# Loads of the gate vectors and of the S5 readout moved to the queue of POOL, with seven gate pairs ahead of the first projection in place of five and the readout's steps spread further

## The chip, the cores and the metric

The kernel runs on one core of a Trainium2 chip. A core has five engines that run their own instruction streams in order: PE (matrix products, with a separate loader for the stationary operand), DVE (element-wise work), ACT (activations and copies), POOL (element-wise work, general) and SP (here it only starts DMA transfers). Sixteen DMA engines are shared by all queues. An engine that starts a transfer puts it on its own queue and goes on; an engine that meets an instruction whose data isn't there stops, with all that stands behind it. The metric is the device time of one execution in microseconds (us); lower is better.

## The reference

One layer of a generator's backbone, on 512 latent tokens and 256 context tokens, width 2048. Cut to its core:

```python
s_c = silu(c)
mx = split(s_c @ w_ada + b_ada, 6)            # 6 vectors of 2048: the adaLN rows
h_lat = modulate(rms_norm(x, g_pre_mix), mx[0], mx[1])
u_lat = h_lat @ w_in                          # first projection, 512 x 2048 x 2048
y = sum of two directions of s5_readout(s5_scan(u_lat[..., 1536:]))   # SSM heads, 512 channels
ssm = gelu(y + d * u); ssm = ssm * sigmoid(ssm @ w_glu)
mix_lat = concat([multiscale_pool(u_lat[..., :1536]), ssm]) @ w_out
x = x + mx[2] * rms_norm(mix_lat, g_post_mix)
f_lat = conv_glu_ffn(modulate(rms_norm(x, g_pre_ffn), mx[3], mx[4]), w_up, w_conv, w_down)
x = x + mx[5] * rms_norm(f_lat, g_post_ffn)
```

`mx[2]` to `mx[5]` are called the gates here. They are products of a vector with a matrix of 2048 columns each, and nothing but the silu of `c` goes into them, so the kernel may compute them whenever there is room.

## The kernel before

Weights are fp32 and come as pages of 128x1024 (512 KB). Each page is split into a rounded part and a remainder: the DMA brings `raw` (issued by SP, L60), ACT makes `whi` (L77), DVE makes `wlo` (L78), and PE runs three matmuls per tile (`mm3`, L176 to L178). `raw`, `whi` and `wlo` have two buffers each, so PE can only start a page when DVE has written its `wlo`. A page that PE uses for 24 matmuls of 512 columns is the usual unit; the text counts pages from the first of the first projection, which is page 8 (pages 8 to 31 first projection `ub`, 32 to 39 pooling, 40 to 60 output projection `wo`, 61 and 62 the GLU weights `glu`, then the rest of the output projection, `wo2`/`wq`, up to page 73).

Work that isn't weights is written as generators and threaded between the pages by a planner (class `Threads`): `tick` is called a few times per page, and lets each generator go on while the page it asked for has come and while the charge of its steps (`yield charge, lag`) fits into 0.76 of the time ticked. So the tables of charges and lags set the order of the instructions, which is then fixed on every engine. `bg.finish(t)` emits all that is left of a generator at one place.

The two generators that matter:

- `gemv` computes three of the gates. One step takes a page `gv` of 128x1024 of the matrix (`gvload`, L172, two buffers, loaded two products ahead) and multiplies it on DVE into a sum (L943). The first `2 * NGP` of these products are done ahead, in the adaLN stage, from loads of 1 MB (`gpair_load`, `gpair_dot`, L607). `gfin` closes a gate (L953 to L959). A second generator loads 32 pages for the fourth gate during the MLP, with the same `gvload`.
- The readout of the SSM runs in `scan`, after the states are ready, in eight units u = 0 to 7. For each: six POOL operations build a table `cl` (`cl_build`, L562 and L564, after a small L786); ACT copies parts of it into `R` (`window`, L797 to L799); PE makes `eb` (L821) and ACT copies it to `E` (L823); DVE adds `du` to a part of `E` (L827); ACT's queue writes `E` to DRAM (`e_scratch`, L828); the queue reads it back in another layout as `Mi` (L810); PE makes `yb` from `cl` and `Mi` (`y_unit`, L760 to L762), ACT applies the gelu (L763); after each second unit PE transposes (`ytp`, L772), and ACT and DVE make `yTr` (L777, L778).

`second_half()` emits the GLU matmuls at page 61 and calls `bg.finish` on what is left of the readout first. Behind the output projection, the normalisation for the MLP (`norm_pair`, from L1056 on) calls `bg.finish` on `gemv` before it forms the MLP's input `hf` and `h` (L1125 to L1130), since that uses two of the gates (`acol`). Then come the MLP's matmuls `up` and `dn`.

Of the kernel before, what the change touches and what calls it, by code (L numbers as in the profile page):

```python
# [129 lines left out]
def emit(tc, A, out, xs_dram, dbg=None):  # L130
    nc = tc.nc
    V, S, PO, PE = nc.vector, nc.scalar, nc.gpsimd, nc.tensor
# [7 lines left out]
    e_dram = nc.dram_tensor("e_scratch", (8, 32, 960), F32, kind="Internal").ap()  # L140
# [19 lines left out]
    def pg(name, shape=(1024,), dt=F32, parts=128):  # L160
        return shaped(sb.tile([128, 1024], dt, name=name, tag="pg", bufs=NPG), shape, slice(0, parts))

    def bank(name, cols=512, parts=128):
        t = ps.tile([128, 512], F32, name=name, tag="bank")
        return t[:parts, :cols]
# [3 lines left out]

    def gvload(ap, q=None):  # L170
        r = ring.tile([128, 1024], F32, name="gv", tag="gv", bufs=2)
        nc.sync.dma_start(r[:], ap)  # L172
        return r

    def mm3(o, ahi, alo, bhi, blo, start, stop):
# [253 lines left out]
    def at(r, f):  # L429
        rounds.setdefault(r, []).append(f)  # L430
# [169 lines left out]
    def gpair_load(nt):  # L600
        gpair[nt] = p0.tile([128, 2, 1024], F32, name="adag", tag="adak", bufs=3)
        nc.sync.dma_start(gpair[nt][:], A["ada_n"][0, nt].rearrange("a p n -> p a n"))

    def gpair_dot(nt):
        g = gpair.pop(nt)
        for hf in range(2):
            V.scalar_tensor_tensor(scr[:], g[:, hf], 1.0, srow[:, hf * 1024:(hf + 1) * 1024], op0=OP.mult,  # L607
                                   op1=OP.mult, accum_out=gacc[:, hf, 0, nt:nt + 1])

    NGP = 5  # L610
    at(31, cond_rows)
    for nt, r in enumerate((34, 36, 38, 40, 42)):
        at(r, lambda nt=nt: gpair_dot(nt))
    for nt, r in enumerate((32, 33, 34, 36, 38)):
        at(r, lambda nt=nt: gpair_load(nt))
    at(4, lambda: W.load(2))
    at(6, lambda: W.make(2))
# [62 lines left out]
    def front():  # L680
# [5 lines left out]
        for gb in range(4):  # L686
# [5 lines left out]
                                        ap=[[768, 8], [6144, 16], [1, 768]]), uc.rearrange("p i c -> p (i c)"))  # L692
        mi_next(NMT)
        yield 0.0, 1.2
        for gb in range(4):
            u = pg(f"UT{gb}", (8, NCH))
            UT[gb] = u
            nc.sync.dma_start(u, bass.AP(tensor=u_dram.tensor, offset=gb * 128 * 768,
                                         ap=[[96, 8], [6144, 16], [768, 8], [1, 96]]))
# [80 lines left out]
        def cl_build(u):  # L780
            g4 = slice(4 * u, 4 * u + 4)
            cu = pc.tile([128, 2, 4, 16], F32, name="cu", tag="cu", bufs=3)
            nc.sync.dma_start(cu[:], A["ssm_c"][:, :, g4, :])
            du = pc.tile([128, 16], F32, name="du", tag="du", bufs=3)
            nc.sync.dma_start(du[:], A["ssm_d"][u])
            PO.tensor_tensor(du[:], du[:], hmask[:], op=OP.mult)  # L786
            cl = [pc.tile([128, 4, 8, 16], F32, name=f"cl{r}", tag=f"cl{r}", bufs=3)[:] for r in range(2)]
            cm = p1.tile([128, 528], F32, name="cm", tag="ps2", bufs=2)
            for _ in cmul_build(cl[0], cl[1], cu[:, 0], cu[:, 1], POUT, 4 * u, 4, PO, cm[:, :512]):
                pass  # L790
            cls[u] = (cl, cu, du)
# [8 lines left out]

        cl_build(0)
        cl_build(1)
        yield 0.0, 1.5
        window(0)
        yield 0.0, 0.5
        for u in range(9):
            if u > 0:
                mi = pc.tile([128, 4, 8, 16], F32, name="Mi", tag="Mi", bufs=2)
                Mis[u - 1] = mi
                nc.sync.dma_start(mi[:].rearrange("p g j h -> p g (j h)"),  # L810
                                  bass.AP(tensor=e_dram.tensor, offset=(u - 1) * 32 * 960,
                                          ap=[[16, 8], [960, 16], [240, 4], [1, 128]]))
            if u < 8:
                du = cls[u][2]
                E = pc.tile([128, 15, 16], F32, name="E", tag="E", bufs=2)
                eb = bank("eb", 240)

                for r in range(2):
                    for g in range(4):
                        c = 512 * r + 16 * (4 * u + g)  # L820
                        PE.matmul(eb[32 * g:32 * g + 32], BBt[:, c:c + 32], R[r][:, g].rearrange("p m h -> p (m h)"),  # L821
                                  start=(r == 0), stop=(r == 1))
                S.activation(E[:].rearrange("p m h -> p (m h)"), eb, AF.Copy)  # L823
                if u < 7:
                    window(u + 1)
                yield 0.0, 0.4
                V.tensor_tensor(E[:, 7, :], E[:, 7, :], du[:], op=OP.add)  # L827
                nc.scalar.dma_start(bass.AP(tensor=e_dram.tensor, offset=u * 32 * 960,  # L828
                                            ap=[[240, 4], [960, 32], [1, 240]]), E[:].rearrange("p m h -> p (m h)"))
            if u > 0:  # L830
                y_unit(u - 1)
            if u + 2 < 8:
                cl_build(u + 2)
            if u > 0 and u % 2 == 0:
                yield 0.0, 0.5
                yt(u // 2 - 1)
            yield 0.0, 0.4

    yT, yTr = [None] * 2, [None] * 4
    mixT = [None] * 16  # L840
# [94 lines left out]
    def gemv():  # L935
        todo = [(c, n, hf) for c in range(3) for n in range(16) for hf in range(2)][2 * NGP:]
        tiles = []
        for x in range(len(todo)):
            while len(tiles) < min(x + 2, len(todo)):
                c, nt, hf = todo[len(tiles)]  # L940
                tiles.append(gvload(A["ada_n"][c, nt, hf]))
            c, nt, hf = todo[x]
            V.scalar_tensor_tensor(scr[:], tiles[x][:], 1.0, srow[:, hf * 1024:(hf + 1) * 1024], op0=OP.mult,  # L943
                                   op1=OP.mult, accum_out=gacc[:, hf, c, nt:nt + 1])
            tiles[x] = None
            gv_state[0] = 2 * NGP + x + 1
            if nt == 15 and hf == 1:
                gfin(c)
            yield 1.8, 0

    def gfin(c):
        a = acol[:, c, :]
# [123 lines left out]
    def norm_pair(rep):  # L1076
# [33 lines left out]
        for kk in range(8):  # L1110
# [21 lines left out]
            yield 1.8 * (kk % 2), 0  # L1132

    fr_t = bg.add(front(), 0)
    gv_t = bg.add(gemv(), 3)
    pb_t = []
# [78 lines left out]
    def gemv5():  # L1215
        for hf in range(2):
            sr = p2.tile([128, 1024], F32, name="srow2", tag="srow2", bufs=1)
            nc.sync.dma_start(sr[:], A["c_row"][:, hf * 1024:(hf + 1) * 1024])
            S.activation(sr[:], sr[:], AF.Silu)
            for nt in range(16):  # L1220
                r = gvload(A["ada_n"][3, nt, hf])
                yield 0.0, 1
                V.scalar_tensor_tensor(scr[:], r[:], 1.0, sr[:], op0=OP.mult, op1=OP.mult,
                                       accum_out=gacc[:, hf, 3, nt:nt + 1])
                yield 1.2, 0
        gfin(3)
        yield from rows_of(3, frow, p2, "srow2", 1)
# [134 lines left out]
    r = None  # L1362
    for t in range(4):
        os = {d: bank(f"df{d}") for d in (2, 3)}
        gps = []
        for d in (2, 3):
            for j in range(2):
# [3 lines left out]
                for k in range(2):  # L1371
                    g = gt[NP - GRP + 2 * j + k]
# [16 lines left out]
        r = rows_rstd(st8[:, t:t + 1, :], 0, 4)[0]  # L1389
# [88 lines left out]
```

## Time and profile before

| | us |
|---|---|
| median of three runs | 2201.22 (2198.22 to 2202.09) |
| the profiled execution | 2198.28 |
| its span in the trace | 2196.5 |
| PE busy | 2074.5 (94%) |
| DVE busy | 1536.8 (70%) |
| ACT busy | 691.5 (31%) |
| POOL busy | 283.1 (13%) |

The span runs from the first to the last instruction; the profiled execution is 1.8 us longer than it. The mean granted clock of TensorE was 0.971. In order of time the stages are: adaLN to 165 us, first projection to 329 us, pooling to about 350 us, output projection with the scan's readout to 545 us, GLU and the rest of the output projection to about 620 us, normalisation to 741 us, MLP to 2143 us, and the end. A stage in which PE is busy throughout has its time set by the matmuls; the places where it is not are where other engines set it.

### The profile page before, as it was taken

The page shows a single profiled execution, that of the slowest core. Times are in us where ns is not written, and L with a number is a line of the kernel's source. Part 1 is how long each engine was busy: PE and PEld are TensorE (multiplying, and loading weights), DVE is VectorE, ACT ScalarE, POOL GpSimd, SP SyncE. Part 2 cuts the span into 40 slices and gives each one's busy share as a digit, 9 for nine tenths or more (in the row PEclk, how much of TensorE's full clock was granted, in tenths as well). Part 3 has the DMA queues.
Part 4 walks back from the last instruction along what each step waited for, and adds up shares of the span by engine and source line. Part 5 has one row for each costly group of instructions (what it writes and reads, how often), then busy time and mean ns, then how long its engine had stood idle before and what let it go on. Part 6 is the DMA issues. An engine that isn't in the chain of part 4 may idle for free.

```text
span 2196.5 us, 24458 instructions
## 1 busy us (share of the span) xinstructions
PE 2074.5 (94%) x9468; PEld 1642.0 (75%) x9468; DVE 1536.8 (70%) x2119; ACT 691.5 (31%) x969; POOL 283.1 (13%) x334
## 2 busy tenths in 40 slices
PE   7998999888955999999999999999999999999996
PEld 3576877666745888888888888888888888888885
DVE  1575798654666688777777777777867767767676
ACT  4343424543435323322222222222222222222224
POOL 5951100571023100000000000000000000000004
PEclk8899999899977999999999999999999999999998
DMA  9876423665655233433333433334323333333335
GB/s 379 302 292 209 163 79 113 212 193 196 239 211 201 76 94 96 144 121 115 120 114 115 134 114 117 115 115 125 105 87 91 93 95 96 96 96 90 93 96 191
DMA packets 94324, 315.00 MB, mean 143 GB/s; under 512 B 17024, under 2 KB 22912, under 8 KB 89984
## 3 DMA queue, kind: packets, MB, share of 16 engines
q1 hardware_dynamic: 90880, 306.07, 42.2%
q10 hardware_dynamic: 3328, 7.37, 1.0%
q8 instruction: 74, 1.21, 0.2%
q14 instruction: 42, 0.34, 0.0%
HBM read 302.46 MB, written 10.94 MB: 143 GB/s over the span
## 4 chain that ended last, share of the span: by engine, by line
PE 66%; DMA 5%; DVE 3%; ACT 2%; issue 1%; POOL 1%; DVEq 0%; SPq 0%; ACTq 0%; POOLq 0%
PE up L177 14%; PE up L176 14%; PE up L178 14%; PE dn L176 7%; PE dn L178 7%; PE dn L177 7%; DMA gv<-in_ada_n 2%; DVE scr L943 1%; DMA raw<-in_w_up 1%; DMA Mi<-e_scratch 1%; ACT scr L1057 1%; DMA e_scratch<-E 1%; PE uh L178 0%; DVE wlo L78 0%; ACT whi L77 0%
## 5 line engine op out<-in xcount | busy, mean ns | idle before, releaser
L78 DVE TENSOR_TENSOR wlo<-raw,whi 128x1024 fp32r<-128x1024 f32 (+1 forms) x326 | 404.0, 1240 | 396.7 <-ACT whi L77 393.6
L77 ACT ACTIVATE whi<-raw 128x1024 fp32r<-128x1024 f32 (+1 forms) x326 | 341.2, 1047 | 741.1 <-PE dn L178 313.1
L1244 DVE SCALAR_TENSOR_TENSOR cv<-zp,wconv,cv 128x512 f32<-128x512 f32 x704 | 528.2, 750 | 18.8
L176 PE MATMUL up<-h,whi 128*128 128x512 f32 x1344 | 531.3, 395 | 0.0
L177 PE MATMUL up<-h,whi 128*128 128x512 f32 x1344 | 530.9, 395 | 0.0
L178 PE MATMUL up<-h,wlo 128*128 128x512 f32 x1344 | 530.6, 395 | 0.0
L177 PEld LDWEIGHTS up<-h,whi 128*128 128x128 f32 x1344 | 252.0, 187 | 61.5
L178 PEld LDWEIGHTS up<-h,wlo 128*128 128x128 f32 x1344 | 251.9, 187 | 61.6
L176 PEld LDWEIGHTS up<-h,whi 128*128 128x128 f32 x1344 | 251.9, 187 | 61.5
L176 PE MATMUL dn<-whi,g 128*128 128x512 f32 x672 | 265.6, 395 | 0.0
L178 PE MATMUL dn<-whi,g 128*128 128x512 f32 x672 | 265.6, 395 | 0.0
L177 PE MATMUL dn<-wlo,g 128*128 128x512 f32 x672 | 265.3, 395 | 0.0
L1059 POOL TENSOR_TENSOR facc<-facc,frow 128x512 f32<-128x512 f32 x11 | 15.4, 1421 | 1434.8 <-ACT scr L1057 1434.8
L943 DVE SCALAR_TENSOR_TENSOR scr<-gv,srow 128x1024 bf16<-128x1024 f32 x86 | 121.5, 1413 | 73.0 <-DMA gv<-in_ada_n 69.1
L1278 ACT ACTIVATE zp<-up 128x512 f32<-128x512 f32 x84 | 50.4, 600 | 378.4 <-PE up L178 378.4
L178 PEld LDWEIGHTS dn<-whi,g 128*128 128x128 f32 x672 | 126.0, 187 | 31.0
L176 PEld LDWEIGHTS dn<-whi,g 128*128 128x128 f32 x672 | 126.0, 188 | 30.6
L177 PEld LDWEIGHTS dn<-wlo,g 128*128 128x128 f32 x672 | 126.0, 187 | 30.5
L1292 DVE TENSOR_TENSOR facc<-facc,dn 128x512 f32<-128x512 f32 x144 | 92.1, 680 | 0.7 <-PE dn L178 0.7
L178 PE MATMUL ub<-hT,wlo 128*128 128x512 f32 x192 | 77.7, 405 | 8.4 <-DVE wlo L78 8.4
L176 PE MATMUL wo<-whi,mx 128*128 128x512 f32 x192 | 80.2, 417 | 0.3 <-ACT whi L77 0.3
L177 PE MATMUL wo<-wlo,mx 128*128 128x512 f32 x192 | 78.1, 407 | 2.2 <-DVE wlo L78 2.2
(274 smaller groups left out, 2453.7 us busy)
## 6 DMA issues: line engine op xcount, KB each, us to landing
raw<-in_w_up SPq DMA_DIRECT2D x176, 512.0 KB
gv<-in_ada_n SPq DMA_DIRECT2D x118, 512.0 KB
raw<-in_w_down SPq DMA_DIRECT2D x88, 512.0 KB
adak<-in_ada_k SPq DMA_DIRECT2D x32, 1024.0 KB
raw<-in_w_out SPq DMA_DIRECT2D x32, 512.0 KB
raw<-in_w_inp SPq DMA_DIRECT2D x24, 512.0 KB
adag<-in_ada_n SPq DMA_DIRECT2D x5, 1024.0 KB
xl<-in_xT SPq DMA_DIRECT2D x8, 512.0 KB
```

The lines of the kernel that those rows point to most:

```text
L77: nc.scalar.activation(hi[:, :n], raw[:, :n], AF.Copy)
L78: nc.vector.tensor_tensor(lo[:, :n], raw[:, :n], hi[:, :n].bitcast(F32), op=OP.subtract)
L176: PE.matmul(o, ahi, bhi, start=start, stop=False)
L177: PE.matmul(o, ahi, blo, start=False, stop=False)
L178: PE.matmul(o, alo, bhi, start=False, stop=stop)
L943: V.scalar_tensor_tensor(scr[:], tiles[x][:], 1.0, srow[:, hf * 1024:(hf + 1) * 1024], op0=OP.mult, op1=OP.mult, accum_out=gacc[:, hf, c, ...
L1057: S.activation(scr[:, :512], m, AF.Square, accum_out=st8[:, t, d:d + 1])
L1059: eng.tensor_tensor(m, m, row[d // 2][:, d % 2, :], op=OP.mult)
L1244: V.scalar_tensor_tensor(a[:], zz, wcol, a[:], op0=OP.mult, op1=OP.add)
L1278: S.activation(zp[j][i % 2][:, 1:9, 1:65], o.rearrange("p (r c) -> p r c", r=8), AF.Copy)
L1292: V.tensor_tensor(f, f, os[t], op=OP.add)
```

## The change

Five edits:

- `gvload` issues its load from POOL's queue unless told otherwise; the second generator of the MLP says `nc.sync` and so stays on SP.
- The read of `Mi` (L810) is issued from POOL's queue, not SP's.
- `NGP` is 7, not 5: four more products (two loads of 1 MB) ahead of the first projection, and four fewer in `gemv`; the rounds in which these loads and products are placed are closer together.
- A product of `gemv` is charged 1.4 us, not 1.8, so that the planner places more of them to a page.
- Three lags of the readout grow: 1.5 to 2.2 pages after the first two `cl_build`, 0.4 to 0.7 after `E`, 0.4 to 0.6 at the end of a unit.

```diff
     def gvload(ap, q=None):
         r = ring.tile([128, 1024], F32, name="gv", tag="gv", bufs=2)
-        nc.sync.dma_start(r[:], ap)
+        (q or nc.gpsimd).dma_start(r[:], ap)
         return r
...
-    NGP = 5
+    NGP = 7
     at(31, cond_rows)
-    for nt, r in enumerate((34, 36, 38, 40, 42)):
+    for nt, r in enumerate((34, 35, 37, 38, 39, 40, 41)):
         at(r, lambda nt=nt: gpair_dot(nt))
-    for nt, r in enumerate((32, 33, 34, 36, 38)):
+    for nt, r in enumerate((32, 33, 33, 34, 35, 37, 38)):
         at(r, lambda nt=nt: gpair_load(nt))
...
         cl_build(0)
         cl_build(1)
-        yield 0.0, 1.5
+        yield 0.0, 2.2
...
-                nc.sync.dma_start(mi[:].rearrange("p g j h -> p g (j h)"),
+                PO.dma_start(mi[:].rearrange("p g j h -> p g (j h)"),
...
-                yield 0.0, 0.4
+                yield 0.0, 0.7
...
-            yield 0.0, 0.4
+            yield 0.0, 0.6
...
-            yield 1.8, 0
+            yield 1.4, 0
...
-                r = gvload(A["ada_n"][3, nt, hf])
+                r = gvload(A["ada_n"][3, nt, hf], nc.sync)
```

How this moves the instructions is seen at three places. The first is the readout on the queues that start its loads. Before, SP carries the pages of weights, the `gv` pages, the inputs of `cl` (L783, L785) and the reads of `Mi`, in this order around units 0 and 1:

```order
L172 DMA gv<-in_ada_n 128x1024 x2
L60 DMA raw<-in_w_out 128x1024
L783 DMA cu<-in_ssm_c 128x2x64
L785 DMA du<-in_ssm_d 128x16
L172 DMA gv<-in_ada_n 128x1024
L810 DMA Mi<-e_scratch 128x4x128
L172 DMA gv<-in_ada_n 128x1024
L60 DMA raw<-in_w_out 128x1024
```

After, POOL carries the `gv` pages and the reads of `Mi` between its own operations; around unit 0 and the third `cl_build` it stands so:

```order
L564 TENSOR_TENSOR cl_3374<-cl_3374,cm 128x512
L172 DMA gv<-in_ada_n 128x1024 x3
L810 DMA Mi<-e_scratch 128x4x128
L172 DMA gv<-in_ada_n 128x1024 x3
L786 TENSOR_TENSOR du<-du,hmask 128x16
L562 TENSOR_TENSOR cl_3515<-cu,pio 128x512
```

So the 12 operations of the first two `cl_build` and the six of each later one now stand in one row with the `gv` loads. In the first projection it is the same on POOL: 17 `gv` loads stand right behind the six operations that build the last but one `mi` table, and 18 behind those of the last; before, no load stood there.

The second place is PE ahead of the GLU. Before, the last pieces of the readout there (the second `yb` of its pair and the transposes) stand between matmuls of the output projection, of which 24 follow:

```order
L762 MATMUL yb<-Mi,UT_1548 64x128
L176 MATMUL wo_3958<-whi,mx_2740 128x512
L177 MATMUL wo_3958<-wlo,mx_2740 128x512
...
L772 MATMUL ytp<-ident,yg_3820 128x64 x8
L176 MATMUL wo_3956<-whi,mx_2734 128x512
L177 MATMUL wo_3956<-wlo,mx_2734 128x512
...
L176 MATMUL glu_4135<-yTr_3553,whi 128x512
```

After, the last three and a half units stand in one piece. It begins with the `yb` of unit 4 and the `eb` of unit 6, and from the `yb` of unit 5 on it reads so (a `yb` is twelve matmuls, of which one or two are shown):

```order
L762 MATMUL yb<-Mi,UT_1507 64x128
L772 MATMUL ytp<-ident,yg_4054 128x64 x8
L821 MATMUL eb<-R_3157,bb 32x240 x4
L821 MATMUL eb<-R_3158,bb 32x240 x4
L760 MATMUL yb<-cl_3930,SN_3101 64x128
...
L762 MATMUL yb<-Mi,UT_1539 64x128
L760 MATMUL yb<-cl_4074,SN_3101 64x128
...
L772 MATMUL ytp<-ident,yg_4054 128x64 x8
L176 MATMUL glu_4194<-yTr_3677,whi 128x512
```

No matmul of the output projection stands in it.

The third place is DVE. Before, products of `gemv` go on past the GLU and between the pages of the last output projection (`wbl`), and 14 more stand in the normalisation:

```order
L1016 TENSOR_SCALAR dg<-ident,acol 128x128 x8
L943 SCALAR_TENSOR_TENSOR scr,gacc<-gv,srow 128x1024
L78 TENSOR_TENSOR wbl<-raw,wbh 128x1024
L943 SCALAR_TENSOR_TENSOR scr,gacc<-gv,srow 128x1024
L78 TENSOR_TENSOR wbl<-raw,wbh 128x1024
L943 SCALAR_TENSOR_TENSOR scr,gacc<-gv,srow 128x1024 x2
L78 TENSOR_TENSOR wbl<-raw,wbh 128x1024
```

After, the last products and the third gate (L958, L959) stand right behind the GLU's pages, and nothing of `gemv` comes later. The rows begin at the GLU's first page (its `wlo` is the first one here):

```order
L78 TENSOR_TENSOR wlo<-raw,whi 128x1024
L943 SCALAR_TENSOR_TENSOR scr,gacc<-gv,srow 128x1024 x2
L827 TENSOR_TENSOR E<-E,du 128x16 x2
L778 TENSOR_TENSOR yTr_4129<-yT_4118,yTr_4129 128x512
L827 TENSOR_TENSOR E<-E,du 128x16
L778 TENSOR_TENSOR yTr_4187<-yT_4118,yTr_4187 128x512
L78 TENSOR_TENSOR wlo<-raw,whi 128x1024
L943 SCALAR_TENSOR_TENSOR scr,gacc<-gv,srow 128x1024 x3
L78 TENSOR_TENSOR wlo<-raw,whi 128x1024
L943 SCALAR_TENSOR_TENSOR scr,gacc<-gv,srow 128x1024 x3
L953 TENSOR_TENSOR acol<-gacc 128x16
L954 TENSOR_TENSOR acol<-acol,colp 128x16
```

Counted over the whole order: between the `wlo` of page 43 (the first page behind the scan) and that of page 61 (the first of the GLU) DVE has 38 products before and 52 after, mostly three to a page where it was two. A unit of the readout comes every second page after, from page 52 to 62, where before it came nearly every page from 52 to 60. Behind the `wlo` of page 64 stand 24 products before and none after. In the whole, `gemv` has 86 products before and 82 after.

## Rows read from the trace of the kernel before

**Rows 1.** Windows: start:end, length, busy time (instructions) by engine, PEclk, DMA share, GB/s

```profile
180.00:200.00 20.00, 14.19 (x46) 10.99 (x46) 12.21 (x20) 2.11 (x2) 0.00 (x0) 0.75 0.72 219
...
640.00:660.00 20.00, 4.17 (x16) 2.99 (x16) 13.29 (x20) 2.90 (x8) 3.47 (x2) 0.50 0.49 157
```

**Rows 2.** Waits of PE over the program: us in total, times, longest

```profile
PE uh L176 <- ACT hf L1125: 22.3, 1, 22.3
PE h2p L1118 <- DVE macc L1056: 17.5, 4, 6.6
PE yb L762 <- DMA Mi<-e_scratch: 12.6, 5, 5.0
```

**Rows 3.** Groups of DVE, 375 to 545 us: busy, mean ns, idle before

```profile
L943 DVE SCALAR_TENSOR_TENSOR scr<-gv,srow 128x1024 bf16<-128x1024 f32 x39 | 57.9, 1486 | 27.6 <-DMA gv<-in_ada_n 27.4
L78 DVE TENSOR_TENSOR wlo<-raw,whi 128x1024 fp32r<-128x1024 f32 x19 | 26.8, 1409 | 30.2 <-ACT whi L77 30.2
```

**Rows 4.** Waits of SP's queue, 372 to 545 us

```profile
SPq L172 <- DVE scr L943: 56.7, 25, 9.8
SPq L810 <- DMA e_scratch<-E: 36.3, 8, 12.2
```

**Rows 5.** Timeline of DVE, two runs of products, `wlo` of pages 43 and 61

```profile
374.26 1.22 DVE L78 TENSOR_TENSOR wlo<-raw,whi 128x1024 fp32r<-128x1024 f32 x1
...
380.39 1.23 DVE L943 SCALAR_TENSOR_TENSOR scr<-gv,srow 128x1024 bf16<-128x1024 f32 x1
...
406.85 1.23 DVE L943 SCALAR_TENSOR_TENSOR scr<-gv,srow 128x1024 bf16<-128x1024 f32 x1 [1.38 <-DMA gv<-in_ada_n]
...
542.13 1.22 DVE L78 TENSOR_TENSOR wlo<-raw,whi 128x1024 fp32r<-128x1024 f32 x1
...
655.98 1.23 DVE L943 SCALAR_TENSOR_TENSOR scr<-gv,srow 128x1024 bf16<-128x1024 f32 x1 [2.38 <-DMA gv<-in_ada_n]
...
669.43 1.23 DVE L943 SCALAR_TENSOR_TENSOR scr<-gv,srow 128x1024 bf16<-128x1024 f32 x1 [1.70 <-DMA gv<-in_ada_n]
```

**Rows 6.** Timeline of POOL: the first two tables of the readout, first and last operations

```profile
409.26 1.11 POOL L562 TENSOR_TENSOR cl<-cu,pio 128x512 f32<-128x512 f32 x1
...
424.84 2.09 POOL L562 TENSOR_TENSOR cl<-cu,pio 128x512 f32<-128x512 f32 x1
...
428.08 1.28 POOL L564 TENSOR_TENSOR cl<-cl,cm 128x512 f32<-128x512 f32 x1
```

**Rows 7.** Chain that ended last, around the GLU and the normalisation: start, length, what

```profile
519.23 6.40 DMA e_scratch<-E
525.69 5.67 DMA Mi<-e_scratch
...
664.99 4.35 DMA gv<-in_ada_n
```

**Rows 8.** Timeline of POOL and DVE in the first projection

```profile
165.00 1.12 POOL L562 TENSOR_TENSOR mi<-bb,pio 128x512 f32<-128x512 f32 x1 [23.34 <-DMA gv<-in_ada_n]
...
173.66 1.30 POOL L564 TENSOR_TENSOR mi<-mi,cm 128x512 f32<-128x512 f32 x1
...
160.17 12.80 SPq L172 DMA_DIRECT2D gv<-in_ada_n  x4
...
163.46 1.23 DVE L607 SCALAR_TENSOR_TENSOR scr<-adag,srow 128x1024 bf16<-128x1024 f32 x1
...
180.15 1.23 DVE L943 SCALAR_TENSOR_TENSOR scr<-gv,srow 128x1024 bf16<-128x1024 f32 x1 [7.54 <-DMA gv<-in_ada_n]
```

**Rows 9.** Timeline of PE: GLU's first matmuls; normalisation and first matmul of the MLP

```profile
544.68 0.40 PE L176 MATMUL glu<-yTr,whi 128*128 128x512 f32 x1
544.91 0.39 PE L177 MATMUL glu<-yTr,whi 128*128 128x512 f32 x1
...
631.35 3.65 PE L1118 MATMUL h2p<-ident,macc 128*128 128x128 f32 x16 [5.89 <-DVE macc L1056]
...
673.12 0.58 PE L176 MATMUL uh<-h,whi 128*128 128x256 f32 x1 [22.30 <-ACT hf L1125]
```

More of the change, by code (lines that the diff above doesn't have):

```diff
@@ L809, in front @@
                 Mis[u - 1] = mi
-                nc.sync.dma_start(mi[:].rearrange("p g j h -> p g (j h)"),
-                                  bass.AP(tensor=e_dram.tensor, offset=(u - 1) * 32 * 960,
+                PO.dma_start(mi[:].rearrange("p g j h -> p g (j h)"),
+                             bass.AP(tensor=e_dram.tensor, offset=(u - 1) * 32 * 960,
                                           ap=[[16, 8], [960, 16], [240, 4], [1, 128]]))
```

## The prediction

> **What bounds the kernel now.** I read the windows first, for the stages in which PE is not busy, then PE's waits, then DVE's groups and SP's waits in the readout, then the timelines of the products, and the chain last. PE's busy time is 2074.5 us of 2196.5, and a page's 24 matmuls go at 0.23 us each [rows 9], 5.6 us a page, so the MLP's time is fixed by matmuls and what can move lies ahead of it. The windows show one deep hole, 640 to 660 us, with 4.17 us of PE in 20 at a granted clock of 0.50, which is 1.2 GHz, and a shallower one at 180 to 200 us [rows 1]. PE's waits name the deep one: `uh`, the MLP's first matmul, waits 22.3 us for `hf`, and the transposes ahead of it 17.5 us for `macc` [rows 2]. `hf` waits for a gate, and that for the last of 14 products of `gemv`. There the reader is to see a pure load rhythm: from 655.98 to 669.43 us five products take 2.69 us each, DVE idle for `gv` ahead of each [rows 5], and the chain runs through `gv` loads of 4.35 us [rows 7]. A product takes 1.23 us of DVE; two buffers, each filled in 4.35 and emptied in 1.23, give (4.35 + 1.23) / 2 = 2.8 us.
>
> Between page 43 (`wlo` at 374.26) and page 61 (542.13) 168 us pass for 18 pages, 101 us of matmuls. DVE lost 27.4 us there to `gv` loads and 30.2 us to `whi` [rows 3]; SP stood 36.3 us ahead of reads of `Mi` that waited for `e_scratch` [rows 4], with `raw` and `gv` loads behind them, and PE waited 12.6 us for `Mi` [rows 2]. These waits are what the changed queues could remove.
>
> **The change, part by part.** The sum is made against the profiled execution, 2198.28 us; the median shown is 2.9 us above it, and I add that at the end.
>
> *Normalisation.* All products are emitted before page 65, so `acol` is ready long before it is used. The transposes then start as they did, at 631.35 us [rows 9], and `uh` follows after a first group and its `hf`, near 633 us, where it was 673.12. That is **-40 us** [-43 to -36]; what is late next is `wlo` and the normalisation's own chain, unchanged.
>
> *Pages 43 to 61.* DVE has 52 products where it had 38, two of them behind page 61's `wlo`, so 50 loads must come through two buffers. The rhythm beside weight pages is (406.85 - 380.39) / 9 = 2.94 us over nine products [rows 5], alone 2.69. Fifty take 147 us, or 134.5. Three per page are 8.8 us against PE's 5.6: the pages wait for DVE, in order behind its products. No pace of the loads seen in the trace covers that; the former waits for `whi` and `Mi` disappear under it, which I count at no further gain.
>
> Now the loads also stand in one row with the `cl` tables on POOL. The first two took 20.1 us together, from 409.26 to 429.36 [rows 6], 10 each beside DVE's work; six operations at the 1.11 to 1.28 of the same rows would be 7. I take 8. While POOL works, no load starts, and DVE lives on two loaded buffers, about 4.4 us of work and landing. The first two tables together, 17.5 us with the small operations between, cost 17.5 - 4.4 = 13; five later ones 8 - 4.4 = 3.6 each, 18. From the end of page 43's `wlo` at 375.5 us: 375.5 + 147 + 31, and 3 for the steps of `E`, give 557 for page 61's `wlo` against 542: **+15 us**. The bounds are 0 (2.69 us a load, all later tables hidden) and +45 (1 us more per load: 50, less 5 of overlap).
>
> POOL's own reads of `Mi`: a table and three loads stand between the write of `E` and the read, so the 6.40 us write [rows 7] is hidden in pages 52 to 60.
>
> *Ahead of the GLU.* The longer lags leave three units to `bg.finish`, and PE has no other matmul there. The chain is: two products ahead of `E`'s addition on DVE, 4; write of `e_scratch` 6.40, read of `Mi` 5.67 [rows 7]; `yb` and transposes, twelve and eight matmuls at 0.23, 4.6 with the gelu beside them; a second write and read, 12.07; the last `yb` at the same pace, 2.6. That is 35.3, where the same place before lost 1.3: **+34 us** [28 to 40]. The write of unit 5 and that of unit 6 start together, so it is two round trips and not three; unit 7's addition stands behind a `yTr` of the pair before it on DVE, which makes the second.
>
> *First projection.* Seven pairs in place of five make the last pair's product end about 5 us later, DVE's four products at 1.23 [rows 8]. POOL's `mi` build starts behind it (165.00 before, right after the last L607) and takes 10 us [rows 8], and now the first `gv` loads stand behind that build: issued near 178 us in place of 160.17 [rows 8]. The third product stood at 180.15 after a wait of 7.54; page 10's `wlo` comes near 195 in place of 182, +13, of which later slack on DVE gives back 5: **+8 us** [+2 to +14; the upper end if the second `mi` build, now between load 17 and 18, costs its 10 us less 4.4 too].
>
> *The rest* (charge, the 32 `gv` loads of the MLP, which stay on SP) has no cost of its own: the MLP's PE covers it, and without that cover a load is 4.35 us once.
>
> The sum: 8 + 15 + 34 - 40 = **+17**, so 2215 us for a profiled execution and about 2218 for the median.
>
> **The price of the new queue.** The trace before has no transfer from POOL, so the latency of one is unknown. Below: nothing, like SP's. Above: POOL operations run 1.11 us alone and 2.09 beside DVE's work [rows 6]; an issue held up so would lose 1 us, which is the +45 above. I take the price at SP's, since a load of 4.35 us is mostly transfer. The Trainium skill, in "DMA: Bandwidth & Descriptors", section "Latency and other measured facts", puts the first byte of a software-generated transfer at about 1 us and of a hardware one at about 0.6. By that, as an estimate, 25 round trips of 0.4 would add 10 us and the sum would be +27; no run before shows it. The same page, "Issuing engines are not separate DMA queues", says that another issuer saves only issue time, on the same 16 engines; the 2.69 us rhythm, with no weights loading on SP, agrees that a free queue alone does not quicken a load.
>
> **Rivals.**
> *Loads land sooner (faster).* If a load free of SP's row lands so that the rhythm is 2.4 us, 50 take 120, 27 less than above; with the tables half hidden page 61 comes 13 us earlier than before, and the sum is 8 - 13 + 34 - 40 = -11: 2190. It decides below 2.6 us a load. For it: SP's 56.7 us of waits for DVE and 36.3 for `e_scratch` [rows 4] go. Against: 2.69 was measured with SP free. A shorter chain ahead of the GLU is not enough alone: with one round trip less, -12, it ends at 2206. Chance 0.24.
> *POOL pays for each load (much slower).* Writing a load's descriptors takes POOL's time, held up beside DVE's products: +30 on pages 43 to 61, and more ahead of the GLU, where three reads of `Mi` stand in a row: 2218 + 30 + 3 = 2251. For it: the 1.11 to 2.09 us [rows 6]. Against: nothing that shows a transfer. The Trainium skill ("SBUF — State Buffer", the box on DVE blocking DMA in "SBUF: two separate sides") says that DVE operations that use both ports keep POOL from writing descriptors; by it the time would go to this rival's, if L943 and L78 are such operations. Chance 0.24.
> *The products were never the limit (same).* If DVE's pages hide the extra products behind the 30.2 us that it waited for `whi`, pages 43 to 61 cost 0 and the chain ahead of the GLU overlaps half: 8 + 0 + 30 - 40 = -2, 2199. Chance 0.10.
>
> **How the numbers follow.** My forecast has 0.42: 2218, its own range 2207 to 2230. A measurement tells about 0.2%, 4.4 us, from no change. Slower takes the forecast and the paying queue, 0.42 + 0.24 = 0.66; faster is the sooner loads, 0.24; same is the last rival, 0.10. The range reaches from the rival of faster loads to past the paying queue: 2188 to 2256, which leaves out about 0.2.
>
> **What would show it.** Right: `uh`'s wait for `hf` of 22.3 us is gone; `wlo` of page 61 about 15 us later than 542; DVE's idle for `gv` in that stretch well above 27.4 us; a hole of PE ahead of the first `glu` of about 35 us with the clock falling in it, its waits `yb` for `Mi`; the third product of the first projection about 13 us later. Wrong: a rhythm of products below 2.6 us or above 3.4; `gv` issues on POOL that last far longer than SP's; the hole ahead of the GLU filled or twice as long; or a `mi` build that does not wait for the last pair.

## The result and the profile after

The changed kernel takes 2261.94 us (median, 2261.78 to 2262.67) where the kernel before, run on the same chip, takes 2201.65: a ratio of 1.0278, 95% interval 1.026 to 1.0295. It is 60 us slower; 2218 was predicted, with a range up to 2256. The span of its profiled execution is 2260.9 us, 64.4 more than before. Below, one execution of 2592.21 us at a granted clock of 0.743 (of the kernel with the gate loads on SP and the old lags) is left out of its median.

Cut at five places of PE and DVE that both traces have, the difference is this (us, from the timelines; "43 to 61" runs from the end of page 43's `wlo` to that of page 61's, "hole" from the end of the last matmul of page 60 to the first `glu`; PE goes over pages 66 to 73 twice, and the cut is the end of the first pass):

| | before | after | difference | predicted |
|---|---|---|---|---|
| end of first projection | 329.1 | 350.5 | +21.4 | +8 |
| 43 to 61 | 167.9 | 212.5 | +44.6 | +15 |
| hole ahead of the GLU | -0.2 | 39.5 | +39.7 | +34 |
| `glu` to the end of the first pass over page 73 | 59.0 | 65.3 | +6.3 | 0 |
| from there to the first `uh` | 69.4 | 27.1 | -42.3 | -40 |
| `uh` to the end | 1523.4 | 1518.5 | -4.9 | 0 |

The last row goes with the products: from `uh` to the end, the runs below with 19 or more products behind page 65 take 1523 to 1528 us, those with four or none 1518 to 1522.

The windows of the changed kernel, read as [rows 1], show holes earlier than before: at 180, 440 and 480 us.

```profile
180.00:200.00 20.00, 5.32 (x21) 4.00 (x20) 5.57 (x8) 1.65 (x2) 6.82 (x9) 0.67 0.62 183
...
440.00:460.00 20.00, 7.15 (x24) 5.42 (x24) 7.58 (x12) 1.06 (x1) 6.05 (x9) 0.66 0.52 162
...
480.00:500.00 20.00, 10.34 (x42) 7.69 (x41) 4.84 (x7) 5.85 (x12) 8.31 (x10) 0.74 0.57 173
```

PE's waits over the program, which answer to [rows 2]:

```profile
PE wo L177 <- DVE wlo L78: 59.1, 12, 16.8
PE yb L762 <- DMA Mi<-e_scratch: 30.5, 7, 11.2
PE ub L178 <- DVE wlo L78: 25.1, 6, 14.7
...
PE uh L176 <- ACT hf L1125: 1.5, 1, 1.5
```

And DVE's for `gv`, after, and then, before the change, the same wait and that of PE for `wlo` in the first projection (that of `wo` was 2.2 us):

```profile
DVE scr L943 <- DMA gv<-in_ada_n: 165.0, 56, 16.9
```

```profile
DVE scr L943 <- DMA gv<-in_ada_n: 69.1, 39, 7.5
PE ub L178 <- DVE wlo L78: 8.4, 3, 4.8
```

So `uh` no longer waits for a gate (1.5 us for 22.3). What came in its place is PE waiting for `wlo` in both projections: DVE stands at a product whose page isn't there, and the `wlo` is queued behind it. Two such waits, the longest and one of the later kind, in DVE's timeline (columns as [rows 5]):

```profile
427.92 2.13 DVE L943 SCALAR_TENSOR_TENSOR scr<-gv,srow 128x1024 bf16<-128x1024 f32 x1
446.99 1.23 DVE L943 SCALAR_TENSOR_TENSOR scr<-gv,srow 128x1024 bf16<-128x1024 f32 x1 [16.94 <-DMA gv<-in_ada_n]
448.26 1.22 DVE L943 SCALAR_TENSOR_TENSOR scr<-gv,srow 128x1024 bf16<-128x1024 f32 x1
...
449.41 1.22 DVE L78 TENSOR_TENSOR wlo<-raw,whi 128x1024 fp32r<-128x1024 f32 x1
...
476.79 2.05 DVE L943 SCALAR_TENSOR_TENSOR scr<-gv,srow 128x1024 bf16<-128x1024 f32 x1 [0.85 <-DMA gv<-in_ada_n]
488.64 1.23 DVE L943 SCALAR_TENSOR_TENSOR scr<-gv,srow 128x1024 bf16<-128x1024 f32 x1 [9.78 <-DMA gv<-in_ada_n]
489.90 1.23 DVE L943 SCALAR_TENSOR_TENSOR scr<-gv,srow 128x1024 bf16<-128x1024 f32 x1
```

And POOL in the same stretch. It issues a load at 423.90, builds two tables, and issues the next two loads at 442.89; the same again around the third table:

```profile
423.90 0.53 POOL L172 DMA_DIRECT2D gv<-in_ada_n  x1 [2.44 <-DVE scr L943]
...
426.88 2.08 POOL L562 TENSOR_TENSOR cl<-cu,pio 128x512 f32<-128x512 f32 x1
...
442.89 1.12 POOL L172 DMA_DIRECT2D gv<-in_ada_n  x2
...
471.93 0.53 POOL L172 DMA_DIRECT2D gv<-in_ada_n  x1 [1.97 <-DVE scr L943]
476.48 0.22 POOL L786 TENSOR_TENSOR du<-du,hmask 128x16 f32<-128x16 f32 x1 [4.01 <-DMA du<-in_ssm_d]
...
483.39 1.26 POOL L564 TENSOR_TENSOR cl<-cl,cm 128x512 f32<-128x512 f32 x1
484.59 1.12 POOL L172 DMA_DIRECT2D gv<-in_ada_n  x2
```

The product at 446.99 starts 4.1 us after the issue, that at 488.64 4.05 after. The profile's list of DMA issues gives a median of 4.5 us from issue to landing over all 82:

```profile
gv<-in_ada_n POOLq DMA_DIRECT2D x82, 512.0 KB, 4.5
```

Once issued, a load lands about as soon as from SP, 4.35 us in [rows 7]. It is issued later.

The hole ahead of the GLU, in PE's timeline (the small rows between are left out), and the reads of `Mi` on POOL:

```profile
615.81 0.38 PE L761 MATMUL yb<-cl,SN 128*64 128x128 f32 x2
627.41 0.69 PE L762 MATMUL yb<-Mi,UT 128*64 128x128 f32 x2 [11.22 <-DMA Mi<-e_scratch]
...
644.63 0.69 PE L762 MATMUL yb<-Mi,UT 128*64 128x128 f32 x2 [7.52 <-DMA Mi<-e_scratch]
...
650.03 0.50 PE L176 MATMUL glu<-yTr,whi 128*128 128x512 f32 x1
```

```profile
620.25 1.26 POOL L564 TENSOR_TENSOR cl<-cl,cm 128x512 f32<-128x512 f32 x1
622.33 1.12 POOL L810 DMA_DIRECT2D Mi<-e_scratch  x1 [0.82 <-issue]
625.60 1.05 POOL L810 DMA_DIRECT2D Mi<-e_scratch  x1 [2.15 <-DMA e_scratch<-E]
639.04 1.03 POOL L810 DMA_DIRECT2D Mi<-e_scratch  x1 [12.39 <-DMA e_scratch<-E]
```

Two long waits for `Mi`, as predicted, with a mean granted clock of 0.78 over 610.5 to 650.

In the first projection, POOL (answering to [rows 8]) starts the `mi` build 11 us later than before and the first gate loads at 183.99, not 160.17:

```profile
175.97 2.15 POOL L562 TENSOR_TENSOR mi<-bb,pio 128x512 f32<-128x512 f32 x1 [33.66 <-DVE up L650]
...
183.99 1.33 POOL L172 DMA_DIRECT2D gv<-in_ada_n  x2
...
250.21 0.53 POOL L172 DMA_DIRECT2D gv<-in_ada_n  x1 [0.74 <-DVE scr L943]
253.77 1.11 POOL L562 TENSOR_TENSOR mi<-bb,pio 128x512 f32<-128x512 f32 x1 [3.03 <-PE mtp L582]
...
263.89 0.59 POOL L172 DMA_DIRECT2D gv<-in_ada_n  x1
```

### The profile page after: what moved, and what is told of

Read it like the earlier page. It is cut to its first block, busy times and chain, and to the rows that moved or that the text cites. A ratio compares the mean times of both kernels' runs of the same rounds, so it can differ in the third digit from the quotient of the medians.

```text
span 2260.9 us, 24490 instructions
## 1 busy us (share of the span) xinstructions
PE 2089.1 (92%) x9468; PEld 1653.0 (73%) x9468; DVE 1528.3 (68%) x2119; ACT 690.3 (31%) x969; POOL 320.9 (14%) x424
## 4 chain that ended last, share of the span: by engine, by line
PE 63%; DVE 2%; ACT 1%; DMA 1%; issue 1%; POOL 0%; DVEq 0%; ACTq 0%; SPq 0%; POOLq 0%
PE up L177 14%; PE up L176 14%; PE up L178 14%; PE dn L176 7%; PE dn L178 7%; PE dn L177 7%; ACT scr L1057 0%; PE uh L177 0%; PE uh L178 0%; PE uh L176 0%; DMA raw<-in_w_up 0%; DMA raw<-in_w_down 0%; DVE facc L1059 0%; DMA rawb<-in_w_up 0%; DVE wlo L78 0%
## 5 line engine op out<-in xcount | busy, mean ns | idle before, releaser
L78 DVE TENSOR_TENSOR wlo<-raw,whi 128x1024 fp32r<-128x1024 f32 (+1 forms) x326 | 403.0, 1237 | 356.4 <-ACT whi L77 353.4
L1244 DVE SCALAR_TENSOR_TENSOR cv<-zp,wconv,cv 128x512 f32<-128x512 f32 x704 | 528.4, 751 | 18.8
L1059 POOL TENSOR_TENSOR facc<-facc,frow 128x512 f32<-128x512 f32 x11 | 15.4, 1423 | 1434.6 <-ACT scr L1057 1434.6
L943 DVE SCALAR_TENSOR_TENSOR scr<-gv,srow 128x1024 bf16<-128x1024 f32 x82 | 104.5, 1274 | 165.7 <-DMA gv<-in_ada_n 165.0
L177 PE MATMUL wo<-wlo,mx 128*128 128x512 f32 x192 | 84.8, 441 | 59.1 <-DVE wlo L78 59.1
L177 PEld LDWEIGHTS wo<-wlo,mx 128*128 128x128 f32 x192 | 40.3, 210 | 74.2 <-DVE wlo L78 65.2
```

What stands on the lines that cost most here:

```text
L78: nc.vector.tensor_tensor(lo[:, :n], raw[:, :n], hi[:, :n].bitcast(F32), op=OP.subtract)
L177: PE.matmul(o, ahi, blo, start=False, stop=False)
L1059: eng.tensor_tensor(m, m, row[d // 2][:, d % 2, :], op=OP.mult)
L1244: V.scalar_tensor_tensor(a[:], zz, wcol, a[:], op0=OP.mult, op1=OP.add)
```

## The experiments

Three theories were held against each other. The row: a load loses time because it is issued behind POOL's tables. The price: a transfer from POOL is dearer by itself. The count: three products a page cost the time whatever the queue. A "burst" in some expectations is the piece of the readout that stands alone ahead of the GLU, where the hole is. A label that begins with a_ is a run made from the changed kernel, one with b_ from the kernel before. Times are medians; ratios are to the kernel before on the same chip.

**The gate loads back on SP, the rest of the change kept (a_gv_sp).**

```diff
-        (q or nc.gpsimd).dma_start(r[:], ap)
+        (q or nc.sync).dma_start(r[:], ap)
```

> The kernel after, with the gate loads back on SP's queue and the reads of Mi left on POOL's. Theory of the row (the loads cost time because they stand in one row with POOL's tables, a transfer from POOL itself costs what SP's costs): the first projection comes back by 15 to 20 us, pages 43 to 61 by 25 to 35 (no load waits for a table, three products per page at 2.9 us stay), the hole of 39 us ahead of the GLU stays: 2262 - 50 = 2212 us, between 2205 and 2222. Theory of the price (each transfer from POOL is dearer by itself, tables hidden): 82 loads at 0.2 to 0.5 us, 2262 - 16 to - 41, and the long waits of DVE of 9 to 17 us behind tables would stay. Theory of the count (three products a page are the cost, whatever queue): 2255 or more.

Measured: 2209.83 us, 1.0031 (1.002 to 1.0042). The row's number; 52 us of the change's 60 go with this one line. The first projection ends at 336.5 (14 sooner), pages 43 to 61 take 172.5 (40 less), and the hole grows by 6.6, with the same products in the same places. (Counted again in both traces, DVE runs 51 there, 38 before; the 52 told ahead took in the one before page 43.) The count as the whole cost falls too, since 172.5 is only 4.6 over before; what the products cost alone is seen further down (b_charge).

**The six operations of each table done twice (a_cl2).** The tables' values stay; POOL works longer.

```diff
-            for _ in cmul_build(cl[0], cl[1], cu[:, 0], cu[:, 1], POUT, 4 * u, 4, PO, cm[:, :512]):
-                pass
+            for _ in range(2):
+                for _ in cmul_build(cl[0], cl[1], cu[:, 0], cu[:, 1], POUT, 4 * u, 4, PO, cm[:, :512]):
+                    pass
```

> The kernel after, with the six POOL operations of each of the eight tables done twice over (the same values are written again). Theory of the row: each of the first two tables holds the gate loads up by 8 us more, each of the five that follow at pages 52 to 60 too, and the last one, which stands in the chain ahead of the GLU: 7 x 7.5 = 52 on pages 43 to 61, 2262 + 52 = 2314, between 2300 and 2325. Theory of the price or of the count (what costs is each transfer from POOL, or the three products a page, and tables hide beside them): 2262 to 2275.

Measured: 2315.59 us, 1.0519 (1.0505 to 1.0533). Of the 54 us more, 44.7 fall on pages 43 to 61 (257.2 for 212.5) and 11 on the hole (50.8 for 39.5). POOL after the first tables, then the next load:

```profile
422.50 0.53 POOL L172 DMA_DIRECT2D gv<-in_ada_n  x1 [2.47 <-DVE scr L944]
...
455.21 1.12 POOL L172 DMA_DIRECT2D gv<-in_ada_n  x2
```

32.7 us between two issues, where it was 19. This shows the row directly: seven tables of 7 us more (six operations of 1.10 to 1.26) cost 44.7, almost one for one, so little of a table is hidden.

**Only the reads of `Mi` back on SP (a_mi_sp); then both kinds of load (a_all_sp).**

```diff
-                PO.dma_start(mi[:].rearrange("p g j h -> p g (j h)"),
+                nc.sync.dma_start(mi[:].rearrange("p g j h -> p g (j h)"),
```

> The kernel after, with only the reads of Mi back on SP's queue. Theory of the row: the reads stand behind tables nowhere that matters, so little: the read lands some 2 us sooner (5.7 for 7.8), twice in the hole ahead of the GLU, and SP's pages of weights wait for e_scratch again: 2262 - 4, between 2250 and 2268. Theory of the price: the five reads of 512-byte pieces are what POOL pays for; 2262 - 15 or more.

> The kernel after with both kinds of load on SP again: what is left is seven pairs, the charge of 1.4 us and the longer lags. Theory of the row: with the gate loads on SP the reads of Mi on POOL cost little at these lags (they did beside POOL's gate loads too, where their return to SP gave nothing), but SP's reads keep its pages of weights waiting for e_scratch: within 8 of the kernel with only the gate loads on SP, 2202 to 2218 us. Theory of the price for Mi (a read from POOL lands in 7.8 us, from SP in 5.7): two reads in the piece ahead of the GLU, 4 us, 2206.

Measured: 2262.1 us for the reads alone (1.0269, 1.0251 to 1.0286), no change; 2191.75 for both (0.9955, 0.9938 to 0.9972). The second was missed: 2202 to 2218 was expected. With the gate loads off POOL the reads' queue is worth 18 us: 11 on pages 43 to 61 and 6 in the hole. PE's waits for `Mi` of the whole program, with the reads on POOL (39.9) and on SP:

```profile
PE yb L762 <- DMA Mi<-e_scratch: 39.9, 6, 13.0
```

```profile
PE yb L762 <- DMA Mi<-e_scratch: 15.8, 5, 6.1
```

Beside POOL's gate loads the larger wait takes its place: with the reads alone back on SP, PE waits 21.6 us for `Mi` in place of 30.5, and 68.0 for `wlo` in `wo` in place of 59.1. Without either queue move, what is left of the change is faster than the kernel before.

**The same two moves, each alone on the kernel before (b_gv_pool, b_mi_pool)** (the diffs are the change's own lines).

> The kernel before, with only the gate loads on POOL's queue (the MLP's 32 stay on SP). Theory of the row: the mi build and the tables stand ahead of loads, so the first projection loses 10 to 18 us and each table 7 us more than before, the first two 14: some 7 x 5 + 14 = 50 in the readout, of which the waits for whi that were there before cover 15 to 20; 2202 + 14 + 32 = 2248, between 2230 and 2265. Theory of the price: 86 loads at no more than 0.2 us, since those of the changed kernel landed in 4.2 to 4.5 us: 2202 to 2219.

> The kernel before, with only the reads of Mi on POOL's queue, the lags as before. Theory of the row: at these lags a read stands right behind a table (as in the kernel with gate loads on SP and the old lags, whose PE waited 53 us for Mi where 21 was seen with reads on SP), so PE waits some 30 us more for Mi and pages 43 to 61 take 195 to 200 in place of 168: 2202 + 28 = 2230, between 2215 and 2240. Rival (SP freed of the 36 us that it stood ahead of these reads, so pages of weights and gates come sooner): 2195 or less.

Measured: 2259.36 us (1.0252, 1.023 to 1.0274) for the gate loads and 2223.88 (1.0101, 1.0087 to 1.0115) for the reads. Both totals are as the row has them, the terms not all. With the gate loads pages 43 to 61 cost the 32 us expected, but the first projection 5.9 where 14 was in the sum, and the normalisation, which was not in it, 13 (82.2 for 69.4), where loads stand behind POOL's L1059. With the reads pages 43 to 61 take 190.7, and PE waits 31.6 us for `Mi`, 12.6 before: 19 more, not 30.

**The lags as before, in the changed kernel (a_lags).**

```diff
-        yield 0.0, 2.2
+        yield 0.0, 1.5
...
-                yield 0.0, 0.7
+                yield 0.0, 0.4
...
-            yield 0.0, 0.6
+            yield 0.0, 0.4
```

> The kernel after, with the three lags of the readout as before. The readout then ends by page 59 in the order and no piece of it stands alone ahead of the GLU. Theory of the burst: the hole of 39 us goes, but the tables and reads of Mi come closer together and POOL's row now waits for e_scratch with gate loads behind, which gives 10 to 20 back: 2262 - 39 + 15 = 2238, between 2225 and 2250. Rival (the two round trips are only moved, since the readout's chain ends at the same time whatever the order): 2262 within 6.

Measured: 2254.68 us, 1.0233 (1.0218 to 1.0248). Neither number: the hole is gone (-0.2), but pages 43 to 61 take 243.1, 31 more, twice what the theory gave back. The reads of `Mi` now stand close behind tables and loads in POOL's row, and PE waits between 380 and 610 us as follows:

```profile
PE yb L762 <- DMA Mi<-e_scratch: 50.6, 7, 9.2
```

**Lags as before, gate loads on SP (a_gv_sp_lags)** (reads still on POOL).

> The kernel after, with the gate loads on SP and the lags as before: what is left of the change is seven pairs, the charge of 1.4 and the reads of Mi on POOL's queue. Theory of the row and the burst: no table ahead of a load, no piece ahead of the GLU, no product in the normalisation, pages of weights not behind the reads of Mi: 2202 - 40 + 15 = 2177, between 2162 and 2190. Theory of the count: 2202 or slower.

Measured: 2225.92 us, 1.0108 (1.009 to 1.0126). Missed by 49: the reads alone, dense behind tables, make pages 43 to 61 227.8 long, with 53.5 us of PE's waits for `Mi`. It was this run that showed the second move to cost by itself.

**The charge: back to 1.8 in the changed kernel (a_charge; the diff the other way round), and 1.4 alone on the kernel before (b_charge).**

```diff
-            yield 1.8, 0
+            yield 1.4, 0
```

> The kernel after, with a product charged 1.8 us again: 38 products between pages 43 and 61 as before, 19 behind page 65, and four units of the readout in one piece ahead of the GLU, not three. Theory of the count: pages 43 to 61 come back by 13 x 2.9 = 38 us, the normalisation waits for products again (+36), the piece ahead of the GLU is longer by one round trip (+12): 2262 - 38 + 36 + 12 = 2272, between 2255 and 2285. Rival (tables, not products, set pages 43 to 61): only 15 come back there: 2295.

> The kernel before, with only the charge of a product at 1.4 us: 51 products between pages 43 and 61 and 4 behind page 65, loads and reads on SP, the readout spread over pages 50 to 59, nothing of it in one piece ahead of the GLU. Theory of the row and the burst (the idea of doing the products sooner was good, what lost was the queue and the lags): the normalisation gives 30 to 40 us, pages 43 to 61 cost 10 to 20 since three products a page at 2.9 us are 8.8 against 5.6: 2202 - 35 + 15 = 2182, between 2168 and 2195. Theory of the count (three products a page lose all that the normalisation gains): 2202 within 5, or slower.

Measured: 2276.13 us (1.033, 1.0315 to 1.0346) and 2183.46 (0.9913, 0.9895 to 0.9932). Both totals as the theory had them. In the first, pages 43 to 61 take 171.8, 41 less, the normalisation 69.6 and the hole 53.7; the first projection ends 8.4 sooner, for which the theory had no term. In the second the way from the first pass over page 73 to `uh` is 27.6 us for 69.4; pages 43 to 61 give back 27.7 (195.6), more than the 10 to 20 expected, and the stretch behind the GLU 12. This is the fastest median of all runs, 0.9% below the kernel before.

**The pairs: five in the changed kernel (a_ngp5), seven alone on the kernel before (b_ngp7)** (`NGP` and its two lists of rounds).

> The kernel after, with five gate pairs ahead of the first projection in place of seven. Theory of the row: POOL's mi build starts some 5 us sooner, and the first gate loads with it; four more products come later, in the normalisation (4 x 2.7 = 11): 2262 - 5 + 8 = 2265, between 2255 and 2272. Rival (the extra 2 MB are what delays the first projection by 21 us, not POOL's build): 2262 - 20 + 8 = 2250.

> The kernel before with only the seven pairs. Theory: two more loads of 1 MB and four products on DVE put the first projection's beginning off by 2 to 7 us, whatever queue the gate loads have, and four of the 23 products behind page 65 go, 4 x 2.7 = 11 us in the normalisation: 2202 + 5 - 11 = 2196, between 2190 and 2202. Rival (the loss of 7 us was POOL's late start only): 2191 or less.

Measured: 2256.62 us (1.0242, 1.0221 to 1.0264) and 2195.28 (0.9967, 0.9954 to 0.9981). Beside POOL's gate loads two pairs fewer end the first projection 6.7 us sooner (343.8); alone, seven pairs move its end by 0.8 (329.9). So the pairs cost through POOL's late `mi` build, and save 11 us in the normalisation where the products are still last there (58.0 for 69.4). In the changed kernel, where they are not, four products more behind page 65 cost nothing there (27.4 for 27.1), against the 11 of the expectation.

**One lag between, and the GLU two pages later.** The charge alone with 0.6 in place of 0.4 after `E` (c_charge_lag); that kernel with `GLU = 5` in place of 3 (charge_lag_glu5); and the changed kernel with both loads on SP and `GLU = 5` (all_sp_glu5).

```diff
-                yield 0.0, 0.4
+                yield 0.0, 0.6
```

```diff
-    GLU = 3
+    GLU = 5
```

> The kernel before with the charge of 1.4 us, all loads on SP, and one lag changed a little: 0.6 in place of 0.4 after E, so that a unit comes every 1.5 pages and one unit's second half stands ahead of the GLU. If the wait for Mi is what the denser order costs (21 us of PE with the charge alone): pages 43 to 61 come back by 10 to 15, the piece ahead of the GLU costs 12 to 18: 2176 to 2192, beside 2183 with the charge alone. If spacing is worth nothing: 2195 to 2200.

> The kernel before with the charge of 1.4 us and the lag of 0.6 after E (2189 us, 21 us of hole ahead of the GLU), and the GLU two pages later; no piece of the readout then stands alone. Theory of the missing cover: 15 to 21 us of the hole go: 2172, between 2166 and 2180. Rival: 2189 within 5.

> The changed kernel with both kinds of load on SP (2192 us, 40 us of hole ahead of the GLU), and the GLU with its two pages of weights two pages of the output projection later. Theory of the missing cover: one unit of the readout moves out of the last piece, beside the two pages, and the hole shrinks by 10 to 20 us: 2192 - 15 = 2177, between 2168 and 2184. Rival (the two round trips begin only with the forced end, wherever it stands): 2192 within 5.

Measured: 2188.86 us (0.994, 0.9926 to 0.9953), 2195.14 (0.9969, 0.9958 to 0.9981) and 2190.79 (0.995, 0.9937 to 0.9962). The first lies in its range; 2172 and 2177 were missed, and of the two rivals only the third run's (2192 within 5) held. The lag alone gives 18.8 back on pages 43 to 61 (176.8) and loses 21.2 to the hole: a move. The later GLU gains nothing clear either: the second is slower by its intervals, the hole goes, and the last output projection waits for the GLU's result instead:

```profile
PE yb L762 <- DMA Mi<-e_scratch: 18.0, 5, 9.4
PE wq L176 <- ACT mx L1005: 10.2, 3, 9.1
```

In the third the hole shrinks by 8 us and the output projection up to the first `wq` is 14 us shorter (240.7 for 255.1), but 10 come back between there and `uh` (60.6 for 50.8), of which the waits for `mx` show only 3.5; the rest stays open. So cover in the order was not enough here; that the readout's chain of writes and reads itself comes too late is the likely reason, and no run separates it.

## Why the prediction was wrong

**Right.** The normalisation: -42.3 for -40, by the step named, and the charge alone shows it (b_charge). The hole ahead of the GLU: 39.7 for 34, two round trips; the excess lies between and behind the round trips, in the steps forecast at 4.6 and 2.6 us, which took 7.7 (from the first `Mi` to the write at 635.09) and 5.4 (from the last `Mi` to `glu`). About 3.5 of these 5.9 us are the clock's, an estimate from the timeline: after two waits in which PE stood idle, the rows of its small matmuls followed each other every 0.43 us at a granted clock of 0.50, which is 1.2 GHz (627.4 to 631 and 644.6 to 648 us), where the same rows stand 0.22 apart at 1.00 (631 to 637). The rhythm of loads between tables, predicted at 2.94, is near 2.9 (2.86 over the five intervals from 411.33 to 425.61 us).

**The step that failed** is in the part on pages 43 to 61: "While POOL works, no load starts, and DVE lives on two loaded buffers, about 4.4 us of work and landing", and "five later ones 8 - 4.4 = 3.6 each". The mechanism was right and the size wrong. From 476.79 to 489.90 two products took 13.1 us, where the rhythm has 5.9: 7.2 for this table. Over the five later tables it is 5.6 to 9.0, in the mean 6.7, nearly twice the term: 34 us for 18. DVE waited for its load at 56 of the 82 products, so it had hardly any stock to live on, and behind the table stands one full landing of 4.1 us before the next product. For the first two tables 13 was predicted and 20.3 - 5.9 = 14.4 measured. That makes 16 + 1.4 = 17 of the 30 us missing here. The run with both kinds of load on SP (a_all_sp) takes 161.4: so both moves together cost 51 us in the changed kernel, of which 31 were in the sum, and the remaining 150 were forecast 11 too low. Of the 51 the gate loads have 40 to 48, as the reads are on POOL or on SP, and the reads of `Mi` 3 to 11, for which the sum had nothing since their writes were taken as hidden. The doubled tables say the same of the row: a microsecond of POOL costs nearly one. The 6.3 us behind the GLU weren't foreseen; no run was made for them, but the charge alone adds 12 there (b_charge).

**The second mis-sized term** is the first projection, +8 with an upper end of 14, measured 21.4. "Ends about 5 us later" was 11 (175.97 for 165.00), and the second `mi` build, kept as an upper end only, held the loads from 250.21 to 263.89. The 11 are not DVE's four products alone: the loads of 1 MB now stand ahead of a page's `raw` on SP's queue, ACT waits for it, and DVE for ACT, with six products behind:

```profile
165.87 1.06 ACT L77 ACTIVATE whi<-raw 128x1024 fp32r<-128x1024 f32 x1 [9.21 <-DMA raw<-in_w_inp]
...
166.96 1.23 DVE L78 TENSOR_TENSOR wlo<-raw,whi 128x1024 fp32r<-128x1024 f32 x1 [5.17 <-ACT whi L77]
```

Undone in the changed kernel, the gate loads' queue gives 14.0 of the 21.4 back, the charge 8.4 and the pairs 6.7; alone on the kernel before they cost 5.9, 3.6 and 0.8. So they add up only together, and the prediction gave the charge no cost here.

**The rivals.** The kernel ended near the rival of a queue that POOL pays for (2251), but not for its reason. A gate load from POOL lands in 4.5 us, and in 4.1 in the run with the reads of `Mi` on SP; from SP in 4.3 and 4.6, in the runs with it back there (medians, SP's with the MLP's 32). The DMA packets of the traces do show a small price: where a gate load's engine had issued nothing for 2 us and its queue was quiet, the first packet starts 1.24 us after the issue from POOL (24 loads of the changed kernel) and 0.96 from SP (13 of the kernel before). The Trainium skill ("DMA: Bandwidth & Descriptors", "Latency and other measured facts") gives 0.4 us more to the first byte of such a transfer; the 0.28 of the traces agrees in kind. Over the prediction's 25 round trips that is 7 us, an estimate, of the 44.6 on pages 43 to 61. What the Trainium skill says in "SBUF — State Buffer" ("SBUF: two separate sides"), of descriptors that POOL can't write while DVE runs an operation in a 2-port mode, isn't seen beside the operations here: the loads from POOL were issued in 0.53 to 0.56 us beside the products (14 of them), in 0.53 to 0.54 beside L78 (22), and in 0.53 to 0.78 with DVE idle. The rival of a count that costs nothing was half right: 13 more products on pages 43 to 61 cost 27.7 us alone, with the shorter lags (b_charge); with the longer lags as well these pages take 4.6 more than before with the gate loads on SP and 6.5 less with both loads there. Two of the rivals' sums don't follow from their words: 27 less on these pages is page 61 13 us sooner with no table hidden at all, and half of the chain ahead of the GLU is 17, not 30.

**The whole by parts.** Alone on the kernel before: gate loads on POOL +58, reads of `Mi` on POOL +22, charge -18, pairs -7. These sum to +55 (each the median less that of before in its own set); the change is +60. That this comes near is luck, since the parts don't add: undone in the changed kernel, the gate loads give back 52, the reads nothing, the pairs 5, and without the charge it is 14 slower. The longer lags, the fifth edit, weren't run alone; undone in the changed kernel they give 7.

## What to carry to other kernels

Moving a load to another engine's queue moves it behind all that this engine computes: count each block of work ahead of a load as a stretch of its whole length plus one landing in which nothing new arrives (here 8 and 4 us), less only what is really in stock, and if the consumer already waits for most loads, next to nothing is. The in-order engine that looks idle (13% busy) isn't a free queue if its work comes in blocks of 8 us and the buffers hold two loads. And make an edit alone: of five here the smallest, a charge in the planner, was worth 18 us, and two others hid it.

## What the runs showed that was not expected

A load of 512 KB issued by POOL lands about as soon as one issued by SP (4.1 to 4.5 us against 4.3 to 4.6), though its first packet starts 0.28 us later and POOL is busy 0.53 us for the issue and 1.07 us for one of `Mi`, where SP took 0.33 and 0.62. Nearly all of the price lies in the order.
